# One 128-slot overflow body under one condition in a mixture-of-experts decoder trunk

## The chip, the core and the metric

The kernel runs on one core of one Trainium2 chip. The metric is the device time of one execution in microseconds. The kernel before took 1218.04 us in the median of three runs (1214.18 to 1219.77).

## What is computed

Two layers. In each, a token-mixing sublayer (retention, pooling and gated delta-rule branches) is followed by a mixture of experts, and each ends in a residual layer norm. The change touches the experts alone. With 256 tokens and 16 experts of hidden width 512:

```
p_g, g_sel = lax.top_k(pc, 1)                      # one of 4 groups
top_w, top_i = lax.top_k(pf, MOE_TOP_K)            # two of the group's 4 experts
for e in range(N_EXPERTS):
    hdn = jax.nn.silu(xt @ w_gate[e]) * (xt @ w_up[e])
    out = out + combine[:, e:e + 1] * (hdn @ w_down[e])
```

Each token weighs in two experts only, so the kernel gathers an expert's tokens and computes those. An expert's float32 weights are 6 MB: four units of 1 MB for gate and up, two for down. The reference's router, evaluated on the run's inputs, gives the experts, in the kernel's order, these numbers of tokens:

- layer 0: 2, 4, 74, 10, 1, 10, 144, 27, 1, 5, 48, 15, 0, 3, 150, 18
- layer 1: 30, 12, 0, 29, 110, 32, 0, 23, 82, 15, 0, 20, 108, 25, 0, 26

## The kernel before

The mixing sublayer ends about 300 us into the span for layer 0 and about 918 us for layer 1. The router's counts (pp) then exist on the chip. Each token of an expert has a position from 1 up (pos, line 850). A selection matrix, made by comparing positions with an index row, gathers tokens by a matmul (gather, lines 872 to 883) and scatters results back.

**Two ways through an expert.** The first 32 slots of an expert are the cheap pass: gate_up (lines 1051 to 1062) runs four column strips of TensorE at once for 32 tokens; four experts (a quad) share one selection (quad_slots), one buffer of gathered tokens and one scatter. Experts with more than 32 tokens need the overflow pass, with a selection of their own (picks on GpSimd, lines 972 to 975). It comes in two sizes: 128 slots, and 64 slots, where two column strips run side by side. The offset `over` (lines 889 to 892) picks the split from the count n:

| n | 32-slot pass | overflow |
|---|---|---|
| 1 to 32 | all | none |
| 33 to 64 | skipped | 64 slots, all |
| 65 to 96 | first 32 | 64 slots |
| 97 to 128 | skipped | 128 slots, all |
| 129 to 160 | first 32 | 128 slots |

Beyond 160 a rare path (again, lines 1121 to 1131) repeats the 128-slot body; it is decided after expert REST = 9 (lines 1164 to 1173) and isn't taken on these inputs.

**The order of an expert** (lines 1137 to 1179) is written by hand. The program is unrolled; a condition is a jump over code, and it is taken on TensorE, VectorE and ScalarE each, from a register that is loaded one expert ahead. Per expert e: slot_rows at e % 4 == 2; gate_up(e) under a condition; a gather for the next quad; by_size (lines 1042 to 1049) around the scatter of the expert before; by_size around over_gather and over_up; picks for e + 1; down(e - 1); turned(e), the transposes of the hidden rows; fetch; by_size around over_down. by_size is an outer condition (line 1043) and within it one for the size (line 1046). So an expert without overflow skips three pieces of code. The scheduler may set the scatter and the gather ahead of the next gate_up. A block under a condition isn't mixed with what stands around it.

**Weights.** A ring of 20 buffers of 1 MB holds units in order; SyncE issues a unit's DMA as soon as the buffer's last reader is done (fetch, lines 954 to 956), and skips experts without tokens (cond, line 222).

The PSUM banks own, other, bank_t and bank_c are shared: bank_c by the gather, slot_rows and the overflow, bank_t by down(e - 1) and the overflow's turned selection (slot_turn). weigh (lines 968 to 970) splits weighted rows into two float32r parts on ScalarE and VectorE, which the scatter adds.

## Time and profile before

| | us |
|---|---|
| median of three runs | 1218.04 |
| lowest, highest | 1214.18, 1219.77 |
| the profiled execution | 1214.9 |
| its span, first to last instruction | 1213.1 |
| mean granted TensorE clock | 0.929 of full speed |

Times in rows are in us from the span's start. PE is TensorE's matmul, PEld its weight load, DVE VectorE, ACT ScalarE, POOL GpSimd; a q behind a name is that engine's sequencer. "L1043" is the line of the code. In a timeline each row has its start, its duration, engine, line, what is written from what, and in brackets the engine's idle time before it and what ended that. In a table by windows each engine has busy us and a count; then come the granted clock as a share of full speed, the DMA engines' busy share and GB/s.

### The profile page before, as it was taken

How to read it: one execution, taken by the hardware profiler on the slowest of the kernel's cores; microseconds unless marked ns; L12 is line 12 of the kernel's file. 1: busy time of each engine (PE TensorE's matmuls, PEld its weight loads, DVE VectorE, ACT ScalarE, POOL GpSimd, SP SyncE). 2: the span in 40 equal slices, each digit the busy share in tenths (PEclk: the TensorE clock that was granted, in tenths of full speed). 3: DMA queues.
4: the chain of work that ended last, by engine and by line, in shares of the span. 5: the costliest groups of instructions: out<-in, count | busy, mean ns of one | idle time of the engine just before them, and what ended most of it. 6: DMA issues, size and time to landing. Idle time of an engine off the chain costs nothing. (4 is left out here: it accounts for less than half of the span.)

```text
span 1213.1 us, 17926 instructions
## 1 busy us (share of the span) xinstructions
PE 1009.7 (83%) x6657; PEld 715.5 (59%) x6657; DVE 466.5 (38%) x980; ACT 400.0 (33%) x680; POOL 180.1 (15%) x224
## 2 busy tenths in 40 slices
PE   7999989998796886758879999899997677684874
PEld 6778678786464443524457777788774444353432
DVE  4786365656211011010167783555674001010013
ACT  4673354452112111011147553544532102111112
POOL 2030030302301110111010400302103110101011
PEclk9999999999898897788989999999998889897888
DMA  9533567568579969196066253766576837957461
GB/s 330 194 118 134 188 229 242 183 215 288 205 283 395 349 236 379 44 390 245 27 224 220 79 182 105 243 243 207 176 259 236 330 150 275 353 209 275 158 235 37
DMA packets 113375, 268.92 MB, mean 222 GB/s; under 512 B 4792, under 2 KB 5216, under 8 KB 113216
## 3 DMA queue, kind: packets, MB, share of 16 engines
q1 hardware_dynamic: 111680, 263.24, 60.6%
q0 software_dynamic: 1248, 3.01, 1.0%
q8 instruction: 102, 1.67, 0.6%
q10 hardware_dynamic: 288, 0.52, 0.1%
q14 instruction: 57, 0.47, 0.1%
HBM read 290.88 MB, written 1.05 MB: 241 GB/s over the span
## 5 line engine op out<-in xcount | busy, mean ns | idle before, releaser
L289 DVE TENSOR_TENSOR W<-R,W 128x1024 fp32r<-128x1024 f32 x148 | 184.3, 1248 | 111.6 <-PE a L295 88.2
L288 ACT CAST W<-R 128x1024 fp32r<-128x1024 f32 x150 | 157.5, 1053 | 166.1 <-PE a L294 148.1
L293 PE MATMUL a<-W,X 128*128 128x512 f32 x504 | 201.5, 401 | 3.7 <-ACT W L288 3.5
L294 PE MATMUL a<-W,X 128*128 128x512 f32 x504 | 199.7, 398 | 0.0
L295 PE MATMUL a<-W,X 128*128 128x512 f32 x496 | 193.6, 397 | 4.1 <-DVE W L289 4.0
L974 POOL TENSOR_SCALAR s_wsm<-cst,s_rrv,s_pos 128x128 f32<-128x128 f32 x64 | 50.2, 792 | 457.0 <-PEq L1043 302.7
L293 PEld LDWEIGHTS a<-W,X 128*128 128x128 f32 x504 | 95.5, 189 | 26.5 <-ACT W L288 4.9
L295 PEld LDWEIGHTS a<-W,X 128*128 128x128 f32 x496 | 93.4, 189 | 26.3 <-DVE W L289 7.5
L294 PEld LDWEIGHTS a<-W,X 128*128 128x128 f32 x504 | 95.2, 189 | 20.6 <-issue 2.3
L1084 ACT COPY yh<-t 32x256 f32<-32x256 f32 x120 | 43.5, 363 | 151.5 <-PE t L1076 148.8
L1076 PE MATMUL t<-M,s_hT 128*32 128x256 f32 x512 | 39.4, 449 | 31.7 <-PEq L1043 17.7
L878 PE MATMUL t<-t,xt 128*128 128x128 f32 x240 | 39.4, 319 | 20.6 <-PEq L1043 12.6
L878 PEld LDWEIGHTS t<-t,xt 128*128 128x128 f32 x240 | 34.6, 223 | 25.9 <-issue 16.8
L1076 PEld LDWEIGHTS t<-M,s_hT 128*32 128x32 f32 x512 | 19.2, 125 | 49.8 <-issue 34.4
L1058 PE MATMUL t<-M,X 128*32 128x256 f32 x512 | 37.1, 442 | 8.7 <-issue 7.5
L1062 DVE TENSOR_TENSOR ul<-ul,t 64x256 f32<-64x256 f32 x16 | 6.8, 424 | 91.4 <-ACTq L1043 50.1
L1061 ACT ACTIVATE ul<-t 64x256 f32<-64x256 f32 x16 | 6.0, 375 | 100.5 <-PEq L1043 60.6
L878 PE MATMUL t<-s_wsm,xt 128*128 128x128 f32 x224 | 32.1, 312 | 7.3 <-PEq L1142 4.3
L1076 PE MATMUL t<-R,s_hT 128*32 128x256 f32 x248 | 22.2, 463 | 18.7 <-DMA M<-in_w_up_dram 10.9
L295 PE MATMUL a<-W,yh 128*128 128x512 f32 x96 | 37.4, 389 | 0.0
L293 PE MATMUL a<-W,yh 128*128 128x512 f32 x96 | 37.4, 389 | 0.0
L294 PE MATMUL a<-W,yl 128*128 128x512 f32 x96 | 37.4, 389 | 0.0
(543 smaller groups left out, 1565.1 us busy)
## 6 DMA issues: line engine op xcount, KB each, us to landing
R<-in_w_in_dram SPq DMA_DIRECT2D x55, 1024.0 KB
M<-in_w_up_dram SPq DMA_DIRECT2D x34, 1024.0 KB
M<-in_w_gate_dram SPq DMA_DIRECT2D x34, 1024.0 KB
M<-in_w_down_dram SPq DMA_DIRECT2D x32, 1024.0 KB
R<-in_w_gate_dram SPq DMA_DIRECT2D x20, 1024.0 KB
R<-in_w_down_dram SPq DMA_DIRECT2D x16, 1024.0 KB
R<-in_w_up_dram SPq DMA_DIRECT2D x14, 1024.0 KB
R<-in_w_branch_dram SPq DMA_DIRECT2D x12, 1024.0 KB
```

Source lines behind the costliest of these rows:

```text
L288: nc.scalar.copy(h, src)
L289: nc.vector.tensor_sub(lo, src, h)
L293: nc.tensor.matmul(acc, hi, wh, start=first, stop=False)
L294: nc.tensor.matmul(acc, lo, wh, start=False, stop=False)
L295: nc.tensor.matmul(acc, hi, wl, start=False, stop=last)
L878: done = nc.tensor.matmul(view[:, i, :], xks[b][:, k, :], picks[b], start=b == 0, stop=b == 1)
L974: last = eng.tensor_scalar(gg[:, b, :], iota, base, pos[:, b, e:e + 1], op0=ALU.add, op1=ALU.is_equal)
L1058: nc.tensor.matmul(p[32 * j:32 * j + 32, 0:256], xg[:, k, es], units[6 * e + j // 2 + 2 * (k // 4)][k % 4][:, c:c + 256], start=k == 0, st ...
L1061: nc.scalar.activation(hh[64:128, 0:256], p[0:64, 0:256], AF.Silu)
L1062: nc.vector.tensor_mul(hh[64:128, 256:512], hh[64:128, 0:256], p[64:128, 0:256])
L1076: done = nc.tensor.matmul(ps[j][32 * j:32 * j + 32, 0:256], hT[:, k // 2, k % 2, :], units[6 * e + 4 + k // 2][k % 2][:, 256 * j:256 * j + ...
L1084: nc.scalar.copy(dst, src)
```

## The change

One condition is left per expert around one body, overflow, that always has 128 slots: gather, up, turned selection, down and scatter in one piece. For n from 33 to 128 it takes all tokens and the 32-slot pass is skipped; for 129 to 160 it takes the first 128 and the 32-slot pass the rest (own_pos = pos - 128). kind is 0, 1, 2 or 3 for n = 0, 1 to 32, 33 to 128, over 128: its low bit says whether gate_up runs, kind > 1 whether overflow does. fetch stands behind overflow and turned; down(e - 1) and turned(e) stand behind the whole overflow. When gate_up is skipped nothing is cleared any more. The 64-slot bodies, slot_turn, over_gather, over_up, over_down, over_scatter and by_size are gone.

```
+WIDE = P + SLOTS
...
+        base, own_pos = small("rrv", [P, 16]), small("rst", [P, 2, 16])
+        nc.vector.tensor_scalar(base, pp[:, 32:48], float(SLOTS), float(P), op0=ALU.is_gt, op1=ALU.mult)
+        nc.vector.tensor_tensor(own_pos, pos, base[:, None, :].to_broadcast([P, 2, 16]), op=ALU.subtract)
...
-        for at in (SLOTS + 64, 64, SLOTS):
-            nc.vector.scalar_tensor_tensor(over, pp[:, 32:48], float(at), over, op0=ALU.is_gt, op1=ALU.subtract)
-        nc.vector.tensor_scalar(over, over, -float(SLOTS), float(SLOTS), op0=ALU.mult, op1=ALU.add)
...
+        nc.vector.tensor_scalar(kind, pp[:, 32:48], 0.0, None, op0=ALU.is_gt)
+        for at in (SLOTS, P):
+            nc.vector.scalar_tensor_tensor(kind, pp[:, 32:48], float(at), kind, op0=ALU.is_gt, op1=ALU.add)
+        nc.vector.tensor_copy(plan, kind)
...
+        def overflow(e, u, own, other):
+            for i, p in enumerate((other, bank_c)):
                 gather(xo[i], [gg[:, b, :] for b in range(2)], list(range(4 * i, 4 * i + 4)), i, p, 0)
+            for j, p in enumerate((other, bank_c)):
+                for k in range(8):
+                    nc.tensor.matmul(p, xo[k // 4][:, k % 4, :], u[j + 2 * (k // 4)][k % 4], start=k == 0, stop=k == 7)
+            nc.scalar.activation(hoT, other, AF.Silu)
+            nc.vector.tensor_mul(hoT, hoT, bank_c)
+            for b in range(2):
+                nc.tensor.transpose(bank_t[:, tbs[b]], gg[:, b, :], ident)
+            for b in range(2):
+                nc.tensor.matmul(bank_t[:, T:T + 1], gg[:, b, :], comb[:, b, e:e + 1], start=b == 0, stop=b == 1)
+            nc.scalar.copy(goT, bank_t[:, 0:T])
+            nc.vector.tensor_copy(wo, bank_t[:, T:T + 1])
+            p = h4(other)
+            for k in range(4):
+                nc.tensor.transpose(p[:, k, :], hoT[:, k * P:(k + 1) * P], ident)
+            nc.scalar.copy(h4(hoT), p)
+            for half, p in enumerate((bank_c, own)):
+                s = sides[half]
                 for k in range(4):
+                    nc.tensor.matmul(p, hoT[:, k * P:k * P + P], u[4 + k // 2][k % 2][:, s], start=k == 0, stop=k == 3)
+                weigh(hi[:, s], lo[:, s], p, wo)
+            for half, s in enumerate(sides):
                 for yy in (hi, lo):
                     for b in range(2):
+                        nc.tensor.matmul(acc[b][half], goT[:, tbs[b]], yy[:, s], start=False, stop=False)
...
-            with tc.If(main > 0) as some:
+            with tc.If((k & 1) > 0):
                 gate_up(e)
-            with some.Else():
-                nc.vector.memset(hh[64:128, 256:512], 0.0)
             if q < 3:
                 gather(xgs[(q + 1) % 2], Gs[q + 1], [2 * (e % 4), 2 * (e % 4) + 1], e, bank_c)
-            if n_before is not None:
-                by_size(n_before, over_scatter)
+            with tc.If(k > 1):
+                overflow(e, units[6 * e:6 * e + 6], own, other)
+            if e + 1 < NE and e != REST:
+                picked = picks(nc.gpsimd, e + 1)
             if e % 4 == 1 and q:
                 weighed(q - 1)
-            by_size(n, lambda n: over_up(e, units[6 * e:6 * e + 6], n, other), lambda: over_gather(other))
-            if e + 1 < NE and e != REST:
-                picked = picks(nc.gpsimd, e + 1, over[:, e + 1:e + 2])
             downed = down(e - 1, hT) if e else done
             with tc.issue_after(downed.ins):
                 hT, placed = turned(own)
             if e % 4 == 1 and q:
                 scatter(q - 1)
-            if e != REST:
-                fetch(6 * e + 4 + held)
-            by_size(n, lambda n: over_down(units[6 * e:6 * e + 6], n, other, own))
-            n_before = n
...
+            fetch(6 * e + 4 + held)
             if e + 1 < NE:
                 with tc.issue_after(placed.ins):
-                    main, n = load(plan[0:1, e + 1, :])
+                    k = load(plan[0:1, e + 1:e + 2])[0]
...
-        by_size(n, over_scatter)
```

The quads' selections compare own_pos instead of pos, and picks starts at 0.

## Rows read from the trace of the kernel before

**Rows 1.** Busy time by windows: the expert stages of layer 0 and layer 1.
```profile
306.00:612.00 306.00, 233.60 (x2037) 138.80 (x2037) 36.92 (x107) 49.80 (x117) 34.83 (x58) 0.88 0.69 256
...
918.00:1213.00 295.00, 203.39 (x1704) 123.07 (x1704) 45.44 (x134) 49.54 (x114) 38.57 (x62) 0.86 0.60 221
```

**Rows 2.** Waits of the whole run: total us, times, longest us.
```profile
PEld t L1076 <- issue: 64.2, 70, 9.6
...
PE t L1076 <- PEq L1043: 27.1, 10, 5.5
...
PE t L878 <- PEq L1043: 12.6, 8, 4.2
...
PE t L1076 <- DMA M<-in_w_up_dram: 10.9, 2, 9.5
```

**Rows 3.** Line 1043 on TensorE's sequencer: count, ns minimum/median/maximum.
```profile
L1043 PEldq COMPARE_BRANCH  x96: 70/219/6277, 316.9 to 1195.1; - x96
```

**Rows 4.** Timeline of TensorE: expert 5 of layer 0, up to expert 6's slot_rows.
```profile
391.06 3.70 PE L1058 MATMUL t<-R,X 128*32 128x256 f32 x64
398.59 3.31 PE L1076 MATMUL t<-M,s_hT 128*32 128x256 f32 x32 [3.84 <-PEq L1043]
...
403.60 0.44 PE L1090 MATMUL t<-cst,t 128*128 128x128 f32 x2 [1.44 <-ACTq L1043]
```

**Rows 5.** The instruction queue from 375 to 407 us: packets, MB, share of engines.
```profile
q8 instruction: 5, 0.08, 1.1%
```

**Rows 6.** The same queue from 564.5 to 599 us, in the overflow of expert 14.
```profile
q8 instruction: 1, 0.02, 0.2%
```

**Rows 7.** Windows: two stretches without overflow, layer 0's five summed, all nine summed.
```profile
360.19:407.05 46.86, 31.14 (x351) 19.42 (x349) 5.39 (x13) 8.97 (x22) 7.36 (x14) 0.87 1.03 390
...
1165.56:1197.37 31.81, 19.95 (x270) 11.44 (x269) 3.46 (x10) 6.82 (x18) 3.13 (x4) 0.89 0.18 62
...
sum 171.40, PE 106.78 PEld 61.86 DVE 19.17 ACT 29.75 POOL 23.20; mean PE 21.36 PEld 12.37 DVE 3.83 ACT 5.95 POOL 4.64
...
sum 332.82, PE 199.98 PEld 118.52 DVE 33.12 ACT 54.87 POOL 47.72; mean PE 22.22 PEld 13.17 DVE 3.68 ACT 6.10 POOL 5.30
```

**Rows 8.** Timeline of TensorE behind expert 9 of layer 0.
```profile
492.94 0.66 PE L1090 MATMUL t<-cst,t 128*128 128x128 f32 x2 [9.78 <-PEq L1142]
```

**Rows 9.** Line 984, slot_turn's loads: count, ns, first and last, forms.
```profile
L984 PEld LDWEIGHTS t<-cst,s_wsm x40: 132/137/192, 345.2 to 1133.9; 128*64 128x64 f32 x24, 128*128 128x128 f32 x16
```

**Rows 10.** Timeline of TensorE: the 128-slot overflow of expert 6, layer 0.
```profile
411.21 3.84 PE L878 MATMUL t<-s_wsm,xt 128*128 128x128 f32 x32
...
429.61 1.07 PE L1076 MATMUL t<-R,s_hT 128*32 128x256 f32 x16
...
431.74 0.66 PE L1016 MATMUL t<-cst,ul 128*128 128x128 f32 x4
...
443.94 1.05 PE L878 MATMUL t<-t,xt 128*128 128x128 f32 x8
```

**Rows 11.** Timeline of TensorE: the 64-slot overflow of expert 2, layer 0.
```profile
341.58 3.74 PE L878 MATMUL t<-s_wsm,xt 128*128 128x128 f32 x32
...
353.43 1.93 PE L1076 MATMUL t<-R,s_hT 128*32 128x256 f32 x32
...
355.46 0.41 PE L1026 MATMUL t<-cst,ul 64*128 64x64 f32 x4
356.61 3.65 PE L1030 MATMUL g<-W,ul 128*64 128x512 f32 x16 [0.73 <-ACT ul L1027]
...
363.79 0.75 PE L1040 MATMUL a<-mix,s_goT 64*128 64x512 f32 x4
...
364.93 1.16 PE L878 MATMUL t<-t,xt 128*128 128x128 f32 x8
```

**Rows 12.** Line 1003, VectorE's product of the overflow: count, ns.
```profile
L1003 DVE TENSOR_TENSOR ul<-ul,t x4: 686/686/687, 429.8 to 1148.6; 128x512 f32<-128x512 f32 x4
```

**Rows 13.** Timeline of VectorE: the first operation of the offset `over`.
```profile
306.54 0.17 DVE L889 TENSOR_SCALAR s_rrv<-t 128x16 f32<-128x16 f32 x1
```

## The prediction

> **What bounds it now.** I read the split by stage first: the two expert stages take 306 and 295 us of the 1213.1 us span, and TensorE is busy for 234 and 203 us of them [rows 1]. So about 70 and 90 us of TensorE idle time lie where the change is. The totals of waits say what ends them: not weights, but "PEq L1043" (TensorE's own sequencer at by_size's outer condition) and "issue" (nothing that the profile shows) [rows 2]. The largest wait put down to weights is 10.9 us, in two times. The conditions have a median of 0.219 us and a longest of 6.277 us [rows 3], so a few of the 96 must cost nearly everything.

> One small expert shows how (expert 5 of layer 0, 10 tokens) [rows 4]. Its gate_up ends at 394.76 us, and the next matmul starts at 398.59: 3.84 us idle for skipping one scatter and one up-projection that no token needs. Then 1.44 us more go to ScalarE's way past over_down's condition, since slot_rows needs bank_c. Over 375 to 407 us, two such experts, 5 packets of 16 KB came on the instruction queue, one per 6.4 us [rows 5]; during a 128-slot overflow, where little is skipped, one came in 34.5 us [rows 6]. So the stalls have the shape of code that must be fetched, skipped code included, at a pace that a small expert outruns. In that stretch the weights moved at 390 GB/s too, a busy share of 1.03 [rows 7].

> Nine stretches hold the 25 experts without an overflow (20 small, 5 without tokens): 332.82 us, TensorE busy for 199.98 [rows 7]. Seven experts overflow.

> **A, the 25 small and empty experts.** Per expert I count TensorE records. A float32 matmul leaves two matmuls and two weight loads, a transpose or float32r matmul one of each. Run: gate_up 64+64, gather 8+8, down 32+32, turned 2+2 = 212. Skipped before: over_gather 64, slot_turn 16 and 32, both up bodies 128, both down bodies 80, both scatters 32 = 352. Skipped after: gather 64, up 64, the turn 12, down 40, scatter 16 = 196. So 564 become 408, a ratio of 0.72, and three conditions become one.
> If the fetch of code set every stretch, all but the pause at expert 9 would shrink by 0.72. That pause, 9.78 us in layer 0 and taken as the same in layer 1, stays [rows 8]. 332.8 - 20 = 313 becomes 225, a gain of 88 us: the strong end. At the weak end only the conditions' own time goes: 64 fewer at 0.22 us, 14 us. Between them I go by the last three experts of layer 1 with the tail, where weights hardly move (share 0.18): 31.81 us, 10.6 each [rows 7]. They hold a wait of the 1.44 us kind, so 9.2 can be reached; the fetch alone gives 225 / 25 = 9.0. Work and fetch will not overlap fully, so I take 9.7: 25 x 9.7 + 20 = 262, **-70 us**.

> **B, the three 64-slot experts.** The loads of the selection, 24 of 64 columns and 16 of 128, at 8 and 4 an expert, say that three took 64 slots and four took 128 [rows 9]. The 128-slot body (expert 6, layer 0): 18.40 from the gather to the end of the up-projection (411.21 to 429.61), and 12.20 for transposes, down and scatter (431.74 to 443.94), together 30.6 us [rows 10]. The 64-slot body (expert 2): 11.85 to the end of up, 1.15 for the transposes and their wait, 3.65 down, 1.14 scatter, together 17.8 [rows 11]. The difference is 12.8, thrice 38.4. Two of the three (64 < n <= 96: experts 2 of layer 0 and 8 of layer 1) also ran gate_up (3.70 us [rows 4]), which the change drops: -7.4. **+31 us**. The body is now in one piece: down(e-1) and turned (2.1 us), which hid VectorE's product behind the up-projection, move behind it, and the turning of the selection takes that place. The product takes 0.69 us [rows 12]; shown whole it would cost seven bodies 5 us. I take 0, since the turning has work for that long. Range +31 to +36.

> **C, the four 128-slot experts.** Same matmuls, other order: 0, bound by the above.

> **D, the rest.** base and own_pos put two VectorE operations (0.17 us each by the nearest row [rows 13], and at most as long again between them) ahead of quad_slots(0) in each layer. TensorE has residual matmuls to run there, so 0 to +1.4 in both, taken +0.5. fetch(e) comes behind the whole overflow; a refill of six units (6.29 MB, 16.1 us at 390 GB/s) then starts some 12 us later (the 12.20 above). It is covered by the lead of twenty units, 54 us by the same rate; if that is used up, the third rival counts. The two picks on GpSimd wait for the same point, and only the next overflow needs them. SyncE's queue is passed by nothing else. The memset in Else is VectorE's and no one waits for it.

> **Sum:** -70 + 31 + 0.5 = -38 us. The profiled execution takes 1214.9 us, 3 below the median of 1218.0; on the median that is **1180 us**.

> **Rivals.** *Conditions cost only their own time* (slower). If the long ones merely sit behind a full TensorE queue, 64 conditions at 0.22 us give 14 back and B stays: -14 + 31 + 0.5 = +18, **1236 us**. The place is the sequencer at L1043; it decides as soon as A gives less than 31 us, 1.2 per expert. For it: the median of 0.219. Against: TensorE is truly idle for 3.84 us there, with gate_up done. [...]
> *Only jumps pay.* If code in sequence costs nothing and each of the three jumps its share of the waits at L1043 (27.1 + 12.6 us in the two largest rows [rows 2]), two thirds go: -26 + 31 + 0.5, about **1223 us**, no change. Against: down's loads wait 64.2 us for "issue" in 70 places [rows 2], and there are 32 downs, so most lie inside one, behind no jump of their own. [...]
> *Weights decide layer 0.* At 16.1 us an expert the loaded stretches of layer 0 could not shrink: its five, 171.4 of the 332.8 us [rows 7], lose their share of A, -36 instead of -70: -36 + 31 + 0.5, about **1214 us**, no change. For it: 390 GB/s in experts 3 to 5 and the 10.9 us of waits. Against: over the whole stage the share is 0.69 [rows 1], so the overflows leave time to refill.
> *The fetch of code sets everything.* -88 + 31 + 0.5 = -56.5, **1161.5 us**. For it: 5 pieces for two experts at 6.4 us each are just their 32 us.

> **How the numbers follow.** A measurement of this kernel tells some 0.5%, 6 us, from no change. The forecast has 0.58, the strong case 0.14, weights 0.08, jumps 0.08, bare conditions 0.12. Faster: 0.57 + 0.14 + 0.02 (weights) + 0.01 (jumps) = 0.74; same: 0.01 + 0.05 + 0.04 + 0.01 (bare) = 0.11; slower: 0.01 + 0.03 + 0.11 = 0.15. The range holds the forecast, the strong case with room below it, and the weights case: 1154 to 1215. It leaves out the bare conditions and the jumps, 0.2. The forecast alone spans 1163 to 1200, from A between its strong end and -50.

> **What would show it.** Right: conditions over 1 us at the remaining If are fewer than one per expert, the nine stretches total some 262 us, the instruction queue shows some 22 packets fewer than now (2.5 an expert by rows 5, times 0.28, for 32 experts), no 64-column loads, 22 gate_ups instead of 24. Wrong on A: stretches near 320 us with long waits left at the If, or waits of TensorE on in_w_gate at the head of experts 5, 6, 9 and 13. Wrong on B: overflow bodies far from 30.6 us. [...]

## The result and the profile after

The changed kernel takes 1166.43 us in the median of four runs (1163.66 to 1171.59), the kernel before 1218.9 in its runs beside them: a ratio of 0.958, 95% interval 0.953 to 0.962. The forecast was 1180 (1154 to 1215), faster. The profiled execution takes 1166.9 us, 48.0 less than that of before, where the sum said 38.

The page of the changed kernel, its head and three queues:

```profile
span 1165.1 us, 17264 instructions
...
q1 hardware_dynamic: 111680, 263.24, 63.0%
...
q8 instruction: 80, 1.31, 0.5%
```

Queue q8 brings code in packets of 16 KB (1.31 MB in 80): 80 where it had brought 102 in the kernel before, 22 fewer, as forecast.

Busy time by windows: first the nine stretches without an overflow, cut at the same places in the code as before, then the seven overflow experts (three that had taken 64 slots, then four that had taken 128, each as a sum).

```profile
365.65:398.43 32.78, 25.32 (x343) 16.12 (x341) 5.14 (x13) 8.90 (x23) 6.95 (x14) 1.00 1.03 382
435.01:472.75 37.74, 22.86 (x319) 13.67 (x319) 4.42 (x10) 7.48 (x19) 6.56 (x14) 0.98 1.04 391
...
1117.59:1149.49 31.90, 23.84 (x279) 13.08 (x277) 4.93 (x12) 9.83 (x24) 2.83 (x4) 0.84 0.63 233
sum 265.68, PE 184.51 PEld 111.15 DVE 35.48 ACT 59.77 POOL 41.88; mean PE 20.50 PEld 12.35 DVE 3.94 ACT 6.64 POOL 4.65
...
sum 107.92, PE 100.83 PEld 57.18 DVE 10.63 ACT 16.37 POOL 5.41; mean PE 33.61 PEld 19.06 DVE 3.54 ACT 5.46 POOL 1.80
...
sum 145.87, PE 137.94 PEld 77.02 DVE 13.90 ACT 19.23 POOL 6.95; mean PE 34.48 PEld 19.26 DVE 3.47 ACT 4.81 POOL 1.74
```

The same two sums of the kernel before:

```profile
sum 80.10, PE 74.23 PEld 49.44 DVE 10.53 ACT 12.17 POOL 5.00; mean PE 24.74 PEld 16.48 DVE 3.51 ACT 4.06 POOL 1.67
...
sum 157.04, PE 144.77 PEld 80.64 DVE 18.97 ACT 22.91 POOL 6.26; mean PE 36.19 PEld 20.16 DVE 4.74 ACT 5.73 POOL 1.56
```

Three of those windows, in layer 1, hold the scatter of a quad (L1107), 2.16 us of it in a former 64-slot one; in the changed kernel these three scatters (L1065) stand in the stretches of layer 1. By windows of that line alone, first in the overflows of the kernel before, then in the stretches of the changed one:

```profile
1056.47:1085.52 29.05, 2.16 (x8) 1.35 (x8) 1.00 0.47 171
...
sum 109.20, PE 6.67 PEld 4.09; mean PE 2.22 PEld 1.36
...
sum 104.24, PE 7.52 PEld 4.85; mean PE 2.51 PEld 1.62
```

Raw, the nine stretches went from 332.82 [rows 7] to 265.68, -67.1, and the overflows from 80.10 + 157.04 = 237.14 to 253.79, +16.7. With the scatters (6.67 us) counted where they stand now, the stretches gave 339.5 - 265.7 = 73.8 us; the three former 64-slot experts, without the scatter of 2.16, cost 107.92 - 77.94 = 30.0 more, the other four, without the other two (4.51), 152.53 - 145.87 = 6.7 less. Elsewhere 2.5 us were added (1.3 ahead of each layer's first gate_up). -73.8 + 30.0 - 6.7 + 2.5 = -48.0.

The third figure from the end of a window's row is the granted clock. Experts 3 to 5 of layer 0 (365.65 on) ran at 1.00 where they had 0.87 [rows 7]. TensorE's busy time in all nine fell from 199.98 to 184.51 us although three scatters came in: the same matmuls ran at a higher granted clock in seven of the nine (0.72 to 0.87 before, 0.81 to 1.00 after), at 1.00 both times in one, and at 0.84 instead of 0.89 in the last. Its idle time there fell by more, from 132.84 to 81.17 us.

TensorE around expert 5 of layer 0, the case of [rows 4], by the timeline:

```profile
386.76 3.66 PE L1016 MATMUL t<-R,X 128*32 128x256 f32 x64
391.87 1.93 PE L1034 MATMUL t<-M,s_hT 128*32 128x256 f32 x32 [1.46 <-PEq L1100]
...
397.34 1.16 PE L883 MATMUL t<-t,xt 128*128 128x128 f32 x8 [0.66 <-DVE s_ce L1052]
...
402.02 3.84 PE L883 MATMUL t<-s_wsm,xt 128*128 128x128 f32 x32
...
421.11 0.66 PE L997 MATMUL t<-cst,ul 128*128 128x128 f32 x4 [0.85 <-DVE ul L988]
...
431.80 1.07 PE L1034 MATMUL t<-R,s_hT 128*32 128x256 f32 x16
```

One pause of 1.46 us at the condition is left of 3.84, and the later 1.44 is gone. At 402.02 expert 6's overflow opens, and at 431.80 the down-projection of expert 5 follows it: 29.8 us for the 128-slot body, forecast at 30.6. The totals of waits say that the cause is thinned out, not gone (L1100 is the overflow's condition, L1096 that of gate_up, to which the two pauses behind expert 9 are put down):

```profile
PEld t L1034 <- issue: 55.0, 59, 6.0
...
PE t L1034 <- PEq L1100: 28.4, 10, 5.8
PE t L1048 <- PEq L1096: 14.9, 2, 9.0
```

### The profile page after: what moved, and what is told of

It is laid out like the page before. It is cut to its first block, busy times and chain, and to the rows that moved or that the text cites. A ratio compares the mean times of both kernels' runs of the same rounds, so it can differ in the third digit from the quotient of the medians.

```text
span 1165.1 us, 17264 instructions
## 1 busy us (share of the span) xinstructions
PE 1014.9 (87%) x6491; PEld 712.4 (61%) x6491; DVE 463.4 (40%) x962; ACT 404.9 (35%) x688; POOL 175.3 (15%) x224
## 3 DMA queue, kind: packets, MB, share of 16 engines
q8 instruction: 80, 1.31, 0.5%
HBM read 290.88 MB, written 1.05 MB: 251 GB/s over the span
## 5 line engine op out<-in xcount | busy, mean ns | idle before, releaser
L296 PEld LDWEIGHTS a<-W,X 128*128 128x128 f32 x496 | 93.6, 189 | 26.3 <-DVE W L290 7.5
L975 POOL TENSOR_SCALAR s_wsm<-cst,s_pos 128x128 f32<-128x128 f32 x64 | 45.6, 721 | 419.4 <-PEq L1100 283.7
L1034 PE MATMUL t<-M,s_hT 128*32 128x256 f32 x512 | 36.8, 419 | 24.9 <-PEq L1100 12.7
L986 PE MATMUL t<-M,zs 128*128 128x512 f32 x112 | 49.2, 595 | 0.0
L988 DVE TENSOR_TENSOR ul<-ul,t 128x512 f32<-128x512 f32 x7 | 4.8, 687 | 93.2 <-PE t L986 93.2
L883 PEld LDWEIGHTS t<-t,xt 128*128 128x128 f32 x240 | 31.7, 206 | 13.3 <-DVE s_ce L1052 5.7
L986 PEld LDWEIGHTS t<-M,zs 128*128 128x128 f32 x112 | 21.0, 190 | 24.9 <-issue 24.6
```

Of the source, the lines that this page charges most:

```text
L296: nc.tensor.matmul(acc, hi, wl, start=False, stop=last)
L883: done = nc.tensor.matmul(view[:, i, :], xks[b][:, k, :], picks[b], start=b == 0, stop=b == 1)
L975: last = eng.tensor_scalar(gg[:, b, :], iota, start, pos[:, b, e:e + 1], op0=ALU.add, op1=ALU.is_equal)
L986: nc.tensor.matmul(p, xo[k // 4][:, k % 4, :], u[j + 2 * (k // 4)][k % 4], start=k == 0, stop=k == 7)
L988: nc.vector.tensor_mul(hoT, hoT, bank_c)
L1034: done = nc.tensor.matmul(ps[j][32 * j:32 * j + 32, 0:256], hT[:, k // 2, k % 2, :], units[6 * e + 4 + k // 2][k % 2][:, 256 * j:256 * j + ...
```

## The experiments

All counts of instructions here are of TensorE, per expert and layer, in the compiled kernels. The kernel before has 180 more than the changed one; 162 more than the one of the first experiment (some texts on record took 180 for both). A piece is a packet of 16 KB, counted as 256 instructions: 201 more in 32 experts brought 25 packets more, 257 to a packet.

**Two by two: code and conditions.** The first kernel is that of before with the 64-slot bodies taken out and all three conditions kept; the second keeps both bodies and merges the three conditions into one.

```
-                with tc.If(n > SLOTS + 64) as wide:
-                    part(n=P)
-                with wide.Else():
-                    part(n=64)
+                part(n=P)
```

> The kernel before with one edit: inside by_size the inner choice goes, and the part with 128 slots runs for every overflow; gate_up still runs for all 27 experts with tokens. So the skipped code of the changed kernel (TensorE has 18 instructions an expert more than it), but still three conditions an expert in the old places. Theory 'code that is fetched': the gain of the changed kernel over the nine stretches without overflow (from 332.82 to 269.78 us in its trace) stays, but for 64 conditions at 0.22 us (14 us); the two gate_ups that stay cost 7.4. From 1166.4 that is about 1188 us, 1175 to 1205. Theory 'jumps': what A gained came with two of the three jumps, so two thirds of the 63 us are lost again, 42, and 7.4 for the gate_ups: about 1216 us, 1205 to 1235.

Measured: 1181.12 us (1176.71 to 1182.08), ratio to before 0.967 (0.962 to 0.973). Its trace has 24 gate_ups, as before, not 27. The 269.78 us in the expectation come from windows of the changed kernel, two of which ended later than those of the kernel before; with ends at the same places it is the 265.68 above.

```
+        def whole(e, u, n, own, other):
+            over_up(e, u, n, other)
+            over_down(u, n, other, own)
+            over_scatter(n)
...
-            by_size(n, lambda n: over_up(e, units[6 * e:6 * e + 6], n, other), lambda: over_gather(other))
+            by_size(n, lambda n: whole(e, units[6 * e:6 * e + 6], n, own, other), lambda: over_gather(other))
```

> The kernel before with its three conditions merged into one: gather, up, down and scatter of the overflow stand in one piece where the changed kernel has them, with the choice between the 64-slot and the 128-slot body inside. So the code of the kernel before (TensorE 13 instructions an expert fewer), one condition an expert. With the run of three conditions and one body it makes a square of two by two. Theory 'code that is fetched': the stretches without overflow stay near 332.82 us less 14 for the conditions, and the overflows cost what they did: 1218.9 - 14 = about 1205 us, 1190 to 1215. Theory 'jumps': the 42 to 63 us of A are won and the longer bodies are not paid for: 1218.9 - 42 to - 63, 1156 to 1177 us, at or below the changed kernel's neighbourhood.

Measured: 1233.82 us (1227.19 to 1237.96), ratio 1.012 (1.005 to 1.019): 1.2% slower than before and outside both ranges, though it has nearly the code of before and 64 conditions fewer. The nine stretches by windows, first of the kernel with three conditions and one body:

```profile
sum 273.41, PE 185.19 PEld 112.20 DVE 32.68 ACT 54.24 POOL 46.75; mean PE 20.58 PEld 12.47 DVE 3.63 ACT 6.03 POOL 5.19
```

then of the one with one condition and both bodies:

```profile
sum 350.87, PE 212.40 PEld 121.74 DVE 36.69 ACT 60.19 POOL 51.92; mean PE 23.60 PEld 13.53 DVE 4.08 ACT 6.69 POOL 5.77
```

TensorE's largest waits in the latter:

```profile
PEld t L1081 <- issue: 149.2, 145, 7.6
PE t L1081 <- PEq L1048: 83.1, 19, 6.7
```

This one, too, has the three scatters of layer 1 in its stretches (L1112, by windows of that line):

```profile
sum 130.07, PE 9.07 PEld 6.26; mean PE 3.02 PEld 2.09
```

So the gain comes with the code. With three conditions the shorter code takes 59.4 us off the stretches, with one 85.2, which is 0.51 us for each of the 167 instructions (180 - 13) that this kernel has over the changed one. With the scatters left out, merging the conditions adds 9.0 us with long code (350.87 - 9.07 - 332.82) and takes 15.2 off with short code (273.41 - 265.68 + 7.52). Jumps as the price are out: with fewer of them the kernel with long code got slower.

**The price of an instruction that nobody runs.** In the changed kernel code was added inside the condition, under a further one that never holds; a small expert jumps over it with the jump that it takes anyway.

```
             with tc.If(k > 1):
                 overflow(e, units[6 * e:6 * e + 6], own, other)
+                with tc.If(k > 3):
+                    for _ in range(1):
+                        overflow(e, units[6 * e:6 * e + 6], own, other)
```

With one body more, 201 instructions:

> The changed kernel with a second overflow body inside its condition, under an inner condition that never holds (kind is 3 at most): 201 instructions of TensorE more for each expert to jump over, which none runs. A small expert takes as many jumps as before; each of the seven overflow experts takes one more. Theory 'code that is fetched': 156 TensorE records an expert were worth 63 us less the 14 of the conditions, 49; 201 then cost about 63 us: 1230, 1205 to 1250, with one packet more on the instruction queue for every 256 instructions, some 25. Theory 'jumps': seven more of them, at most 3.6 us each and 0.2 each by the median: 1168 to 1190 us; and unchanged, 1166, if code that is not run costs nothing.

With three (range(3)), 593 instructions:

> The same with three such bodies: 593 instructions of TensorE more for each expert to jump over. Theory 'all skipped code is fetched at a pace': three times the cost of one body, about 1166 + 186 = 1350 us, 1300 to 1390, and some 75 packets more. Theory 'a jump past what has been fetched ahead starts a new fetch at its target and leaves out what lies between', for which the pause behind expert 9 speaks (some 12 packets of code jumped over in 9.8 us): a small expert pays one wait for a fetch, 6 us or so, whatever the length, 25 times at most and in part instead of the waits it has: 1230 to 1300 us, with hardly more packets than with one body. Theory 'jumps': as with one body.

Smaller doses have one gather of four blocks there instead of a body, or three of them:

> The changed kernel with 38 instructions of TensorE more an expert inside its condition, under an inner condition that never holds: 243 instructions to jump over instead of 205, still under one 16 KB piece of 256. 201 more cost 102 us, over the 59 us that 180 instructions made between the kernel before and the one with three conditions and one body. Theory 'each instruction has its price': by the 102 us, 0.51 us for each instruction an expert, 1186 us, 1178 to 1192. Theory 'a jump of more than a piece always waits for a fetch, a shorter one mostly lands in what was fetched ahead': at most the pace of the code, 25 small experts at 38/256 of 6 us: 1166 to 1178 us with e10 far above it.

> The same with 102 instructions more: 307 to jump over, more than one piece of 256. Theory 'each instruction has its price': 1166 + 52 = 1218 us, 1205 to 1225. Theory 'more than a piece always waits': most of what the whole body cost, 1235 to 1268 us.

| instructions more | us (low to high) | over 1166.4 | per instruction | packets |
|---|---|---|---|---|
| 0 | 1166.43 (1163.66 to 1171.59) | | | 80 |
| 38 | 1187.43 (1185.86 to 1188.68) | 21.0 | 0.55 | 85 |
| 102 | 1225.43 (1223.02 to 1230.17) | 59.0 | 0.58 | 93 |
| 201 | 1268.27 (1258.73 to 1270.99) | 101.8 | 0.51 | 105 |
| 593 | 1306.29 (1303.21 to 1311.38) | 139.9 | 0.24 | 123 |

The packets say whose code q8 brings: 38, 102 and 201 instructions of TensorE for 32 experts are 4.8, 12.8 and 25.1 pieces, and 5, 13 and 25 came. Up to 201 the times are near a straight line, with no step at 256 instructions of a jump: "each instruction has its price" held, the step did not. (In the nine stretches alone, one trace each, an instruction costs 0.57, 0.61 and then 0.36 us, so a bend may begin before 201.) My first figure for 201, 63 us, was too low, and 1268 lies above its range. The size fits the pace of the fetch: the instruction queue of the changed kernel from 435 to 475 us, three small experts and the pause behind expert 9, with weights beside them,

```profile
q1 hardware_dynamic: 6770, 15.46, 102.3%
q8 instruction: 7, 0.11, 1.2%
```

brings a packet every 5.7 us, 22 ns an instruction, and 25 experts without an overflow at that are 0.56 us. The stretches (by windows) took nearly all of it, and TensorE's waits stand where the jump ends. First with 201 instructions, by windows, experts 3 to 5 of layer 0 and the sum of the nine:

```profile
377.76:425.39 47.63, 31.10 (x342) 18.60 (x340) 5.14 (x13) 8.89 (x23) 6.92 (x14) 0.82 1.03 390
...
sum 361.96, PE 213.42 PEld 120.50 DVE 35.05 ACT 58.59 POOL 44.32; mean PE 23.71 PEld 13.39 DVE 3.89 ACT 6.51 POOL 4.92
```

Its waits:

```profile
PEld t L1034 <- issue: 167.2, 138, 11.3
PE t L1034 <- PEq L1100: 91.0, 18, 11.2
```

Of the 96.3 us more in the stretches, 28.9 are TensorE's busy time (184.51 to 213.42) for the same matmuls: at 0.82 of the clock instead of 1.00 in the window shown. How much of that lengthened the run isn't shown: the fetch of 25 x 201 instructions at 22 ns is by itself more than the 96.3 us.

Then with 593, the sum of the nine:

```profile
sum 369.10, PE 218.60 PEld 123.60 DVE 35.46 ACT 58.40 POOL 42.98; mean PE 24.29 PEld 13.73 DVE 3.94 ACT 6.49 POOL 4.78
```

Two of its waits (L1102 is the inner condition):

```profile
PE t L1034 <- PEq L1100: 107.4, 21, 7.8
PE t L1034 <- PEq L1102: 23.0, 7, 3.6
```

Three times the code costs the stretches 7 us more than once the code, and the queue brought 43 packets more, not the 74 that it amounts to: neither theory's count (75, or hardly more than with one body). So with jumps of 798 instructions part of the code jumped over was left out, 43 packets of 74, where jumps of 406 had brought all 25; TensorE waited at the condition all the same (107.4 us in 21 times), and that it waits there for the target of the jump is my reading. 23.0 us are the inner jump over 593 in the seven overflow experts. Nor is the fetch hidden where weights run and little code is executed: 38 instructions cost 21.0 us.

**Who sets the pace.** Two kernels without the refill of the ring in the expert stages; they leave out the loads of all units beyond those held at the start and compute with what lies in the ring.

```
-                expert_unit(len(units))()
+                issue = expert_unit(len(units))
+                if len(units) <= held:
+                    issue()
```

> The changed kernel without the refill of the ring in the expert stages: after the units that are held at their start, no weights of experts are loaded, and the later experts compute with what lies in the ring. The matmuls, the conditions and the code stay. It leaves out some two thirds of the weight traffic there. Theory 'the pace of the code is set by the weight traffic' (packets of code come some 6 us apart where the weights run at 390 GB/s, and 3.1 to 3.6 us apart at the end of layer 1, where they don't): the 25 small experts with 431 instructions, 1.7 packets, want 5.6 us of code at 3.3 us a packet, less than their 7.5 us of TensorE, so the nine stretches go from 265.7 to about 210 us, and the time to about 1110 us, 1095 to 1130. Theory 'the pace is the same whatever the weights do': packets stay 6 us apart and the stretches at 265 us: 1160 to 1167 us, since TensorE waits for no weights there now.

Measured: 1119.5 us (two runs, 1115.75 to 1123.25). This total can't be set against the changed kernel's: with other weights layer 0 gives other values, so the router of layer 1 spreads the tokens otherwise, and the trace has eight overflow bodies (256 matmuls at L988 where the changed kernel has 224) and 21 gate_ups instead of 22. Layer 0 has the same tokens for every expert in both. Its five stretches, summed, in the changed kernel and without the refill:

```profile
sum 126.22, PE 89.77 PEld 53.86 DVE 18.01 ACT 30.22 POOL 21.56; mean PE 17.95 PEld 10.77 DVE 3.60 ACT 6.04 POOL 4.31
...
sum 97.45, PE 84.00 PEld 51.90 DVE 17.85 ACT 30.77 POOL 20.87; mean PE 16.80 PEld 10.38 DVE 3.57 ACT 6.15 POOL 4.17
```

So 28.8 us go there. The timeline of TensorE over expert 4 of layer 0, from its gate_up to the next one, shows where:

```profile
371.59 3.66 PE L1018 MATMUL g<-M,X 128*32 128x256 f32 x64
375.18 1.16 PE L883 MATMUL t<-t,xt 128*128 128x128 f32 x8
377.04 1.93 PE L1036 MATMUL t<-M,s_hT 128*32 128x256 f32 x32 [0.69 <-ACTq L1102]
378.90 0.33 PE L1027 MATMUL g<-cst,ul 64*128 64x64 f32 x2
379.16 3.66 PE L1018 MATMUL t<-R,X 128*32 128x256 f32 x64
```

It takes 7.57 us (371.59 to 379.16) with no wait of TensorE's own sequencer; the 0.69 is ScalarE's way past the condition. In the changed kernel the same expert took 9.66 (377.10 to 386.76), with the weights beside it:

```profile
377.10 3.66 PE L1016 MATMUL g<-M,X 128*32 128x256 f32 x64
381.90 1.46 PE L1034 MATMUL t<-M,s_hT 128*32 128x256 f32 x19 [1.14 <-DVEq L1100]
384.42 1.06 PE L1034 MATMUL t<-M,s_hT 128*32 128x256 f32 x13 [1.06 <-issue]
```

There only 0.2 us of TensorE's waits in the experts are put down to a weight DMA, so I read that the weights act through the code. The run with 201 dead instructions and no refill says it once more:

> The run with one dead body (201 instructions more an expert) without the refill of the ring, so it leaves out the loads of expert weights as the run without refill (1119.5 us) did. Theory 'the price of skipped code is its fetch, and the weights set the pace of that': packets 3 to 4 us apart; 201 instructions are 2.9 us a small expert at 3.7 us a piece, less some 1.3 us of slack that TensorE's own 7.5 us leave over 1.7 pieces: 25 x 1.6 = 40 us, 1160 us, 1145 to 1180. Theory 'the price is that of jumping and has nothing to do with the weights': 102 us as with them, about 1221 us.

Measured: 1177.54 us (1175.13 to 1179.96), 58.0 over the run without refill, whose routing it shares: 0.29 an instruction against 0.51 with weights. Layer 0's five stretches with 201 dead instructions, first with the refill, then without:

```profile
sum 175.23, PE 106.82 PEld 61.19 DVE 17.95 ACT 30.11 POOL 21.53; mean PE 21.36 PEld 12.24 DVE 3.59 ACT 6.02 POOL 4.31
...
sum 123.76, PE 94.78 PEld 56.65 DVE 18.39 ACT 31.09 POOL 21.98; mean PE 18.96 PEld 11.33 DVE 3.68 ACT 6.22 POOL 4.40
```

The dead code costs 49.0 us there beside the weights and 26.3 without them. Over the same three experts (3 to 5 of layer 0, the same code) the instruction queue has, first from 377.76 to 425.39 us with weights, then from 364.56 to 391.75 without,

```profile
q8 instruction: 8, 0.13, 1.1%
...
q8 instruction: 8, 0.13, 1.9%
```

a packet every 6.0 us beside the weights and every 3.4 without, where TensorE is the busier of the two. The transfer of a packet took about the same time (1.1% of 16 engines over 47.63 us and 1.9% over 27.19 are 1.05 and 1.03 us each); what is longer is the time until it comes, and where it waits these runs don't show.

**Does the place of the code matter?** Code was added in the block behind expert 9, which is jumped over in one piece, to move all code behind it against the borders of the pieces.

```
                             again(i, own, other)
+                    gather(xo[0], [gg[:, b, :] for b in range(2)], list(range(4)), 0, other, 0)
```

> The changed kernel with a gather more inside the block behind expert 9 that is only entered when an expert has more than 160 tokens: in each layer 72 instructions of TensorE more in code that is jumped over in one piece in any case. It shifts all code behind it against the 16 KB pieces by 72 instructions (of 256), then by 144 from layer 1's expert 10 on, and leaves the counts alone. Theory 'the amount of code decides': 1166 us within 6. Rival 'where the borders of the pieces fall decides, and the changed kernel merely fell well': over 10 us in either direction.

> The same with two gathers, 104 instructions a layer, so 104 and then 208 of 256. Theory 'amount of code': 1166 us within 6. Rival 'borders': over 10 us in either direction, and another value than with 72.

Measured: 1165.97 (1164.11 to 1166.9) and 1164.98 us (1160.28 to 1170.23). At these two other places the time is the same; that the changed kernel's gain is luck of its layout is unlikely.

**Another cut.** The overflow in two parts around down(e - 1) and turned:

```
+        def overflow_down(e, u, own, other):
             for b in range(2):
                 nc.tensor.transpose(bank_t[:, tbs[b]], gg[:, b, :], ident)
...
+            with tc.If(k > 1):
+                overflow_down(e, units[6 * e:6 * e + 6], own, other)
```

> The changed kernel with its overflow body cut in two under two conditions, around the down-projection of the expert before and the turning: gather and up first, then turn, down and scatter. 8 instructions of TensorE an expert more. Theory 'fetch of code': what is jumped over comes in two pieces of 128 and 68 records with 2.3 us of work between them, on which the fetch can go on; with long code three pieces beat one (332.8 against 350.9 us in the nine stretches), with short code one beat three (265.7 against 273.4). So between the changed kernel and the one with three conditions less its two gate_ups (1181 - 7): 1160 to 1175 us, a little under 1166 if the cover is worth more than the 32 conditions at 0.2 us (7 us). Theory 'jumps': 32 more at a few us for the small ones: 1185 us and more.

Measured: 1178.17 us (1173.16 to 1183.89). A miss: 8 instructions at 0.55 are 4.4 of the 11.7 us, and I had hoped for cover. The other 7.3 are about what 32 conditions at 0.22 us come to (7.0); but the order of the work changed too (the next quad's gather now cuts the down-projection in two), so they are not told apart. That left a question: one piece costs 0.51 to 0.58 an instruction, but between the kernel before and the one with three conditions and one body lie 59.4 us of stretches for 162 instructions, 0.37. The last run put 99 dead instructions (three gathers) into the first of the three conditions of the latter.

> The kernel with three conditions and one body (1181 us) with 99 instructions of TensorE more an expert in its first condition, under an inner condition that never holds: 246 to jump over there instead of 147. In one piece an instruction an expert cost 0.51 to 0.58 us (38, 102 and 201 of them), but from this kernel to the one before, 180 instructions in three pieces cost 40 us in all and 59 in the nine stretches, 0.33 an instruction. Theory 'the same price in every arrangement, and the kernel before is cheap for another reason': 1181 + 54 = 1235 us, 1225 to 1245. Theory 'three pieces with work between them hide part of the fetch': 1181 + 33 = 1214 us, 1203 to 1222.

Measured: 1235.12 us (1232.49 to 1236.75), 54.0 more, 0.55 an instruction. Its stretches by windows:

```profile
sum 324.19, PE 200.93 PEld 120.91 DVE 32.71 ACT 54.40 POOL 48.02; mean PE 22.33 PEld 13.43 DVE 3.63 ACT 6.04 POOL 5.34
```

So three pieces hide nothing of the first, long one. The kernel before has a first piece of about this length, and its other 63 instructions lie in the second and third, short ones; those cost 332.82 - 324.19 = 8.6 us by one trace each, 0.14 an instruction. Why code in the short pieces is that cheap stays open.

## Why the prediction was right

The sum was -38 us and -48.0 came; the mechanism held, and the 10 us between lie mostly in C.

**A, -70: right, -73.8.** The mechanism is as stated: code that is skipped is still fetched (5, 13 and 25 packets more for 4.8, 12.8 and 25.1 pieces of it, in jumps of up to 406 instructions), and its amount, not the number of conditions, sets the small experts. 25 at 9.7 us were forecast with 20 for the pauses behind expert 9, 262; 265.7 came, with three scatters (7.5) in it and 14.9 for the pauses. That leaves 243.3, 9.7 each: the choice between 9.0 and 10.6 held, more closely than the argument could promise. The pauses, taken as staying, gave 5.2 us of the 73.8; before they were

```profile
PE t L1090 <- PEq L1142: 20.1, 2, 10.3
```

The row to lean on was the last three experts of layer 1, where weights hardly moved. They themselves gained little (31.81 us before, 31.90 with a scatter of 2.99 in it), with more refills beside them (DMA share 0.18 [rows 7] to 0.63). That the refills held them back isn't shown: with three conditions and one body these experts took 31.17 us at a share of 0.22. The weak end, bare conditions, was not it. What the 64 conditions themselves gave stays open: three conditions and one body took 14.7 us more than one condition, and two gate_ups (7.4) and 18 instructions at 0.55 (9.9) are more than that.

**B, +31: right, +30.0.** The three bodies took 30.4, 30.3 and 29.8 us against 30.6 forecast and 17.8 for the 64-slot one; less the two gate_ups. VectorE's product stayed covered but for 0.85 us a body, the pause ahead of the transposes. Only 128-column loads of the selection are left, and 22 gate_ups.

**C, 0: the term that was off, -6.7.** I had taken the same matmuls to take the same time. 2.6 us of it is expert 14 of layer 0 alone, whose gate_up by windows before and after is

```profile
559.95:566.21 6.26, 6.26 (x66) 2.88 (x65) 0.32 (x2) 0.37 (x1) 0.00 (x0) 0.57 0.79 311
...
538.68:542.34 3.66, 3.66 (x66) 2.04 (x65) 0.32 (x2) 0.37 (x1) 0.00 (x0) 1.00 1.03 407
```

It ran at a granted clock of 0.57, and then at 1.00. In the 9 us ahead of it TensorE had three waits of 4.7 us in all before, and has one of 1.4 now. That was in reach: the clock of the stretches stood in [rows 7], and the sum has no term for it. The other 4 us are not put down to a cause.

**D, +0.5: 2.5, mis-sized.** 1.3 us ahead of each layer's first gate_up; the bound was 1.4 for both layers together, so it was too low.

**The rivals.** Bare conditions (1236 us): out, by the price that 38, 102 and 201 dead instructions have without a condition more on the short path. Only jumps pay (1223): out, by the kernel with one condition and both bodies at 1234. Weights decide layer 0 (1214): out in the form I gave it. Its five stretches shrank from 171.4 to 15.82 + 32.78 + 37.74 + 29.63 + 10.25 = 126.2 us with the weights at 1.03 or 1.04 of their share in three of them; but the weights do act, by the pace of the code, and without them these five take 97.4. Fetch sets everything (1161.5) came closest to the time, 5 us below the measured median; its own figure for A, -88, was further off than -70, and C made up for it.

## What to carry to other kernels

In this unrolled program code under a condition had a price where it was not run: 20 to 23 ns for each TensorE instruction that a short path jumped over while weights loaded (0.51 to 0.58 us over 25 experts), and about half of that without (26.3 us against 49.0 in layer 0's five stretches), so a second variant of a body must win more where it runs than its length costs all who skip it. The 64-slot body saved each of three experts about 12 us, and with three conditions it cost 25 others 2.4 us each. Look for idle time at a condition with nothing late, count the packets on the instruction queue in that stretch, and try a dose of dead code before counting conditions.
